# Two transformer blocks on one core: rope, masks and residues move from POOL to DVE, and projections stand ahead of attention

## The chip, the cores and the metric

The kernel runs on one core of a Trainium2 chip. The metric is the time of one execution on the device, in microseconds. Five engines work from queues of their own: PE (TensorE, with PEld for its weight loads), DVE (VectorE), ACT (ScalarE), POOL (GpSimd) and SP (SyncE, which here issues DMAs). An engine takes its instructions in the order of its queue; an instruction that waits holds up all that stand behind it.

## The reference

256 tokens of width 1024 pass through two blocks, all in float32. Block 1 adds a mixer and an MLP:

```python
y_a = sliding_window_sink_attention(q_a, k_a, v_a, attn_sinks) @ w_att_up   # 8 query heads, 2 key heads of 64, window 128
ret = chunkwise_retention(q_r, k_r, v_r)                                    # 4 heads, keys 128, values 256
y_r = (silu(g_r) * head_groupnorm(ret, ret_gn_gain)) @ w_ret_up
merged = sigmoid(gate_a) * y_a + sigmoid(gate_r) * y_r
h = h + merged @ w_out
h = h + square(relu(rmsnorm(h) @ w_ff1)) @ w_ff2
```

Block 2 sees 16 meta tokens ahead of the 256, that is 272 keys:

```python
o_swa = windowed_gqa_sink_attention(qa, ka, va, attn_sink, pos, is_real)    # 16 query heads, 4 key heads of 64
o_diff = differential_attention(qb, kb, vb, lam, lambda_init, gain, is_key) # softmax(q1 k1) - lam softmax(q2 k2), 8 heads
merged = g_swa * (o_swa @ w_branch_swa) + g_diff * (o_diff @ w_branch_diff)
h = h + rms_norm(merged @ w_out, post_mix_gain)
h = h + rms_norm((silu(a) * b) @ w_ffn_out, post_ffn_gain)                  # a, b = u @ w_ffn_in
```

A sink is a logit that takes part in the softmax and has no value. `rope` turns halves of each head by tables of cosines and sines.

## The kernel before

All weights stream as 272 units of 512 KB. `next_unit` and `fetch` load a unit as `raw`, ACT casts it to a rounded part `hi` (L300, two instructions of 128x512) and DVE computes the rest `lo` (L302, two of 128x512); a projection is then 24 matmuls a unit, 8 slices of the depth with `hi` against the rounded activations, `hi` against their rest, and `lo` against the rounded ones (`mm_a`, L456). There are 4 buffers of `raw`, 5 of `hi` and `lo`, and the code takes units one ahead.

`rope_T` (L503 to L513) takes a projection: ACT copies it out, ACT's queue issues DMAs that swap the halves into `sw`, DVE multiplies by the cosines (L509), POOL multiplies `sw` by the sines and adds (L510, L513). `stack_q` (L521 to L524) makes of each query its rounded part (ACT) and its rest (POOL) on two halves of the partitions. `stack_k` (L536 to L539) makes of each key head a tile `ks` with the rounded part on both halves and a tile `kl` with the rest, half by DVE and half by POOL.

`scores` (L546 to L549) gives two matmuls for a score tile `s` and, where there is a mask, one or two more that add a bf16 table through an identity. `sink_softmax` puts the sink into a further column (DVE, L560), takes the row's extreme (L554), the exponential with its sum (ACT, L564), the reciprocal (L566) and the normalised `pn` (DVE, L567). `sink_attention` does this for four heads, transposes them into `pt_ps`, splits that into `pt` (L328 ACT, L329 DVE), multiplies with the values into `o_ps` (L586, which has the single PSUM bank `pv`), and folds that by `ol` and `of` into the output's rounded part and rest.

PSUM has two banks `acc` for projections, two `tp` for transposes, two `s` for scores, one `pv`, and one `x` that joins one of these by phase. A scheduler reorders the instructions as it places them by its own estimates, so the order in the queues is not that of the code. In block 2 the code runs, in this order: values, keys for the window heads, then for each of 4 groups `c` the queries and two `sink_attention`; then for each of 4 pairs `pr` keys, queries, two differential heads and one gate; then, in a phase of its own (`b3`), the first branch product `bs_ps` four times, and four times a gate with the second branch product `bd_ps`. Block 1 runs the retention (four heads: `ra`, `at`, `ro`, `ry`, `yt_ps`), keys and values `kv_ps`, two groups of queries `qa_ps` with two `sink_attention` each, then gates and branch products `au_ps` and `ru_ps`.

## Time and profile before

| | |
|---|---|
| median of 3 runs (lowest, highest) | 917.13 us (916.29, 918.17) |
| the profiled execution | 916.17 us, its span 914.4 us |
| busy: PE, DVE, ACT, POOL | 888.0, 626.2, 516.0, 174.5 us |
| granted clock of TensorE, mean | 0.997 of 2.4 GHz |
| retention and block 1's attention | 33 to 208 us |
| block 2: window attention, differential heads, branch products | 465 to 588, 582 to 657, 612 to 697 us |

PE's matmuls are pipelined: the record of one reaches beyond the start of the next, so a step is read from start to start. A busy share is an average of stages with different limits, so the stages are read one by one.

### The profile page before, as it was taken

What the parts mean: (1) busy time and instruction counts of PE and PEld (TensorE: products, weight loads), DVE (VectorE), ACT (ScalarE), POOL (GpSimd) and SP (SyncE); (2) the same over time, 40 slices, a digit from 0 to 9 for tenths busy, and PEclk for the clock granted to TensorE, in tenths of its full rate; (3) what the DMA queues carried; (4) which work ended last, traced back from release to release, by engine and by line L of the source; (5) the groups of instructions that cost most, each with busy time, mean ns of one, the idle gap of its engine ahead of it and who ended that gap; (6) DMA issues with size and microseconds to landing.
All of it is one profiled execution on the core that took longest, in us unless ns stands there. A gap on an engine that the chain in (4) does not pass through costs nothing. (4 is left out here: it accounts for less than half of the span.)

```text
span 914.4 us, 16482 instructions
## 1 busy us (share of the span) xinstructions
PE 888.0 (97%) x6188; PEld 813.1 (89%) x6188; DVE 626.2 (68%) x1201; ACT 516.0 (56%) x1128; POOL 174.5 (19%) x181
## 2 busy tenths in 40 slices
PE   6999899999999999999989999999999999999997
PEld 4899889998899999987989889899999799999996
DVE  5556889677755555575689999988567675655554
ACT  4544357555655544565657788886455564444442
POOL 3013460101000111101273535451011100000000
PEclk9999999999999999999999999999999999999999
DMA  8675454478565666562664343433457566655551
GB/s 279 237 215 175 147 152 138 125 222 297 166 211 190 195 188 185 186 229 84 204 210 134 110 135 111 136 108 116 139 185 225 213 200 200 190 193 186 185 161 46
DMA packets 48126, 160.18 MB, mean 175 GB/s; under 512 B 6432, under 2 KB 8224, under 8 KB 48048
## 3 DMA queue, kind: packets, MB, share of 16 engines
q1 hardware_dynamic: 43376, 153.95, 53.0%
q10 hardware_dynamic: 4672, 5.20, 2.0%
q8 instruction: 48, 0.79, 0.3%
q14 instruction: 30, 0.25, 0.1%
HBM read 151.83 MB, written 2.10 MB: 168 GB/s over the span
## 5 line engine op out<-in xcount | busy, mean ns | idle before, releaser
L302 DVE TENSOR_TENSOR lo<-raw,hi 128x512 fp32r<-128x512 f32 x536 | 380.3, 751 | 190.8 <-ACT hi L300 187.2
L300 ACT CAST hi<-raw 128x512 fp32r<-128x512 f32 x532 | 301.9, 618 | 239.1 <-issue 81.7
L468 PE MATMUL op<-hi,hid 128*128 128x512 f32 x416 | 130.2, 394 | 0.0
L456 PE MATMUL fi_ps<-xf2t,hi 128*128 128x256 f32 x640 | 113.8, 281 | 0.0
L456 PEld LDWEIGHTS fi_ps<-xf2t,hi 128*128 128x128 f32 x640 | 98.6, 188 | 1.0
L468 PEld LDWEIGHTS op<-hi,hid 128*128 128x128 f32 x416 | 76.3, 188 | 16.1
L456 PE MATMUL fi_ps<-xf2t,lo 128*128 128x256 f32 x320 | 89.7, 280 | 0.0
L468 PE MATMUL op<-lo,hid 128*128 128x512 f32 x208 | 81.7, 394 | 0.0
L456 PE MATMUL f_ps<-xf1t,hi 128*128 128x256 f32 x448 | 80.2, 281 | 0.0
L456 PEld LDWEIGHTS f_ps<-xf1t,hi 128*128 128x128 f32 x448 | 69.5, 188 | 1.3
L456 PE MATMUL f_ps<-xf1t,lo 128*128 128x256 f32 x224 | 62.8, 280 | 0.0
L456 PEld LDWEIGHTS fi_ps<-xf2t,lo 128*128 128x128 f32 x320 | 60.4, 189 | 0.0
L456 PE MATMUL q_ps<-x2t,hi 128*128 128x256 f32 x256 | 50.0, 286 | 0.0
L456 PE MATMUL gate_ps<-x1t,hi 128*128 128x256 f32 x256 | 48.4, 285 | 0.0
L456 PE MATMUL gate_ps<-x2t,hi 128*128 128x256 f32 x256 | 48.4, 284 | 0.0
L468 PEld LDWEIGHTS op<-lo,hid 128*128 128x128 f32 x208 | 39.1, 188 | 8.9
L417 POOL TENSOR_SCALAR e<-ss 128x1 f32<-128x1 f32 (+1 forms) x11 | 4.1, 368 | 221.8 <-ACT py L1030 192.7
L797 POOL TENSOR_TENSOR sq<-relu 128x512 f32<-128x512 f32 x14 | 15.8, 1131 | 150.5 <-ACT relu L794 150.5
L456 PEld LDWEIGHTS f_ps<-xf1t,lo 128*128 128x128 f32 x224 | 42.3, 189 | 0.1
L456 PEld LDWEIGHTS q_ps<-x2t,hi 128*128 128x128 f32 x256 | 40.3, 189 | 0.8 <-issue 0.5
L456 PEld LDWEIGHTS gate_ps<-x2t,hi 128*128 128x128 f32 x256 | 39.8, 188 | 0.6 <-issue 0.5
L456 PEld LDWEIGHTS gate_ps<-x1t,hi 128*128 128x128 f32 x256 | 39.8, 189 | 0.2
(297 smaller groups left out, 2015.6 us busy)
## 6 DMA issues: line engine op xcount, KB each, us to landing
raw<-in_wstream_dram SPq DMA_DIRECT2D x272, 512.0 KB, 3.6
sw<-t ACTq DMA_DIRECT2D x40, 64.0 KB, 3.8
x<-in_x_dram SPq DMA_DIRECT2D x3, 512.0 KB, 6.1
sw<-t ACTq DMA_DIRECT2D x40, 34.0 KB, 2.3
sw<-t ACTq DMA_DIRECT2D x8, 128.0 KB, 3.7
g_pre<-in_gains_dram SPq DMA_DIRECT2D x2, 512.0 KB, 7.1
x<-hf SPq DMA_DIRECT2D x2, 512.0 KB, 2.7
x<-x SPq DMA_DIRECT2D x2, 512.0 KB, 6.2
```

Source lines behind the costliest of these rows:

```text
L300: nc.scalar.copy(hi[:, c:c + PIECE], raw[:, c:c + PIECE])
L302: nc.vector.tensor_sub(lo[:, c:c + PIECE], raw[:, c:c + PIECE], hi[:, c:c + PIECE].bitcast(F32))
L417: nc.gpsimd.tensor_scalar(out=e[:np_], in0=ss[:np_, 0:1], scalar1=1.0 / D, scalar2=EPS, op0=ALU.mult, op1=ALU.add)
L456: nc.tensor.matmul(out, wv[a][:, k, j * P:(j + 1) * P], XT[:, b, k, n0:n1], start=(i == 0), stop=(i == last))
L468: nc.tensor.matmul(out, XT[:, b, k0 + k, t0:t1], wv[a][:, k, c0:c0 + cn], start=(start and i == 0), stop=(stop and i == last))
L797: nc.gpsimd.tensor_tensor(out=q, in0=r, in1=r, op=ALU.mult)
```

## The change

- Masks: the table is now f32 (128x800, 400 KB, loaded ahead of weight unit 4) and holds one row block for each kind of score tile. `scores` has no mask matmuls. One DVE instruction (`tensor_tensor_reduce`) adds the mask to the scores, writes them to `pn` and takes the minimum with the sink as its start; it stands in the order as two rows. The sink's column is a copy on POOL of four columns at a time. The normalisation is on ACT.
- Rope: the multiply by the sines and the add are on DVE. The rests of `stack_q` are on DVE.
- `stack_k`: ACT casts once for a pair of heads into `ku` (one buffer), DVE computes its rest, and four DMAs on POOL's queue (64x544 f32, 139 KB each) copy both into the two stacked tiles. There are 11 such stacks, 10 of them in block 2.
- The copy of half of `o_ps` is two ACT copies of 64x256 in place of one of 64x512.
- Order of the code: the window heads' next queries, and the first pair's keys and queries, are projected ahead of the attention of the present ones; those of pair `pr + 1` after the first differential head of pair `pr`. Each pair now has its first gate, its `bs_ps` and its second gate; that gate is kept in `gd`, in the buffers of `pt`. The phase `b3` is gone, and `bd_ps` stands alone at the end. The units of the weight stream are in the new order.

```diff
-    "b2": dict(vt=4, sw=2, t1=2, t2=2, ks=6, kl=6, qe=2, qo=2, p=6, a=2, at=1, atm=2, y=1, pn=2, pt=2),
-    "b3": dict(gt=4),
+    "b2": dict(sw=2, t1=2, t2=2, ks=8, ku=1, qe=2, qo=2, at=2, atm=2, y=2, pn=3, pt=2),
...
         nc.vector.tensor_mul(t1, raw, C)
-        nc.gpsimd.tensor_tensor(out=sw, in0=sw, in1=S, op=ALU.mult)
+        nc.vector.tensor_mul(sw, sw, S)
...
-        nc.gpsimd.tensor_tensor(out=out, in0=t1, in1=sw, op=ALU.add)
+        nc.vector.tensor_add(out, t1, sw)
...
-        nc.gpsimd.tensor_tensor(out=qe[64:128], in0=qf[0:64], in1=qe[0:64].bitcast(F32), op=ALU.subtract)
+        nc.vector.tensor_sub(qe[64:128], qf[0:64], qe[0:64].bitcast(F32))
...
     def stack_k(self, kf, n):
+        u = self.t([P, 2, n], "ku", F32R)
+        nc.scalar.copy(u[:, 0], kf)
+        nc.vector.tensor_sub(u[:, 1], kf, u[:, 0].bitcast(F32))
         r = []
         for e in range(2):
-            nc.scalar.copy(ks[a], kf[a])
-            nc.scalar.copy(ks[b], kf[a])
-            nc.vector.tensor_sub(kl[a], kf[a], ks[a].bitcast(F32))
-            nc.gpsimd.tensor_tensor(out=kl[b], in0=kf[a], in1=ks[a].bitcast(F32), op=ALU.subtract)
+            ks = self.t([P, 2, n], "ks", F32R)
+            for b in range(2):
+                nc.gpsimd.dma_start(out=ks[64 * b:64 * b + 64].bitcast(F32), in_=u[64 * e:64 * e + 64].bitcast(F32))
...
-        for i, (mi, c0) in enumerate(mask or ()):
-            nc.tensor.matmul(out[:, c0:c0 + P], self.identb, self.masks[:, mi * P:(mi + 1) * P],
-                             start=False, stop=(i == len(mask) - 1))
...
-        nc.vector.tensor_copy(s[:, n:n + 1], nsink)
-        nm = self.row_min(s)
+        nc.vector.tensor_tensor_reduce(out=p[:, :n], in0=s, in1=mask, scale=1.0, scalar=nsink, op0=ALU.add,
+                                       op1=ALU.min, accum_out=nm)
...
-        nc.vector.tensor_scalar(out=out, in0=p[:, :n], scalar1=rc, scalar2=None, op0=ALU.mult)
+        nc.scalar.activation(out=p[:, :n], in_=p[:, :n], func=AF.Copy, scale=rc)
...
         for c in range(4):
-            q = self.stack_q(self.rope_T(self.proj_a(XT, name="q_ps"), 2, NTOK, rope_b, 32, scale=-0.125))
+            if c < 3:
+                nq = queries()
+            else:
+                nk, nq = keys(), queries()
             for qt in range(2):
...
         for pr in range(4):
-            kb = keys()
-            q = self.stack_q(self.rope_T(self.proj_a(XT, name="q_ps"), 2, NTOK, rope_b, 32, scale=-0.125))
+            kb, q = nk, nq
             for m in range(2):
+                self.diff_attention(q, kb[2 * m:2 * m + 2], vb, OD, m, 2 * pr + m)
+                if m == 0 and pr < 3:
+                    nk, nq = keys(), queries()
+            mv = MS[:, 2 * pr:2 * pr + 2, :]
+            self.gate(XT, 16, pr, mv)
+            b = self.proj_a(OS, name="bs_ps")
+            nc.vector.scalar_tensor_tensor(out=mv, in0=mv, scalar=1.0, in1=b, op0=ALU.add, op1=ALU.mult)
+            if pr % 2 == 0:
+                gd.append(self.t([P, 4, NTOK], "gd", tag="pt"))
+            self.gate(XT, 24, pr, gd[-1][:, 2 * (pr % 2):2 * (pr % 2) + 2, :])
```

Three places of the order. First, PE near the end of the window attention. A row is a line of the code, an operation, the tile written and those read (their numbers tell one from another), and a shape. Before, at the products of the last but one group (`o_ps_6124`), with a gate's matmuls between:

```order
L456 MATMUL gate_ps_7414<-x2t_2615,hi166_7217 128x256 x2
L456 MATMUL gate_ps_7414<-x2t_2615,lo166_7218 128x256
L456 MATMUL gate_ps_7414<-x2t_2615,hi167_7415 128x256 x2
L456 MATMUL gate_ps_7414<-x2t_2615,lo167_7416 128x256
L456 MATMUL gate_ps_7414<-x2t_2615,hi167_7415 128x256
L586 MATMUL o_ps_6124<-pt_6150,va_4839 128x512
L582 MATMUL pt_ps_6226<-ident_82,pn_6162 128x128 x4
```

After, at the last but three and the last but two group (`o_ps_5663`, `o_ps_5743`):

```order
L586 MATMUL o_ps_5663<-pt_5689,va_4780 128x512 x2
L582 MATMUL pt_ps_5754<-ident_82,pn_5701 128x128 x4
L582 MATMUL pt_ps_5764<-ident_82,pn_5701 16x128 x4
L547 MATMUL s_6301<-ks_5984,qe_6119 128x272
L548 MATMUL s_6301<-ks_5984,qe_6119 128x272
L957 MATMUL vT_ps_5919<-ident_82,vt_5814 16x128 x2
L957 MATMUL vT_ps_5919<-ident_82,vt_5883 16x128 x2
L547 MATMUL s_6307<-ks_5987,qo_6120 128x272
L548 MATMUL s_6307<-ks_5987,qo_6120 128x272
L586 MATMUL o_ps_5743<-pt_5749,va_4780 128x512 x2
L586 MATMUL o_ps_5743<-pt_5759,va_4780 128x512 x2
L957 MATMUL vT_ps_5925<-ident_82,vt_5814 128x128 x2
```

Where `gate_ps` filled the steps between attention matmuls, scores, transposes of values (`vT_ps`) and products now follow each other.

Second, the first queries of block 2: POOL before, DVE before, then DVE after and POOL after. `t1` and `sw` are the rope's operands, `qe` and `qo` the stacked queries, `kl` and `ku` the rests of keys.

```order
L510 TENSOR_TENSOR sw_5104<-sw_5104,rope_b_4725 128x512
L513 TENSOR_TENSOR t1_5105<-t1_5105,sw_5104 128x512
L510 TENSOR_TENSOR sw_5368<-sw_5368,rope_b_4725 128x512
L513 TENSOR_TENSOR t1_5369<-t1_5369,sw_5368 128x512
L523 TENSOR_TENSOR qe_5115<-t1_5105,qe_5115 64x512
L524 TENSOR_TENSOR qo_5116<-t1_5105,qo_5116 64x512
```

```order
L538 TENSOR_TENSOR kl_5028<-t1_5017,ks_5027 64x272
L538 TENSOR_TENSOR kl_5034<-t1_5017,ks_5033 64x272
L509 TENSOR_TENSOR t1_5369<-t2_5370,rope_b_4725 128x512
L302 TENSOR_TENSOR lo146_5868<-raw146_5869,hi146_5867 128x512 x2
L302 TENSOR_TENSOR lo147_5903<-raw147_5904,hi147_5902 128x512 x2
```

```order
L513 TENSOR_TENSOR sw_4954<-sw_4954,rope_b_4666 128x512
L309 TENSOR_TENSOR lo143_5299<-raw143_5300,hi143_5298 128x512
L516 TENSOR_TENSOR t1_4955<-t1_4955,sw_4954 128x512
L309 TENSOR_TENSOR lo144_5331<-raw144_5332,hi144_5330 128x512 x2
L535 TENSOR_TENSOR ku_4880<-t1_4870,ku_4880 128x272
L526 TENSOR_TENSOR qe_4965<-t1_4955,qe_4965 64x512
L527 TENSOR_TENSOR qo_4966<-t1_4955,qo_4966 64x512
```

```order
L573 COPY pn_5217<-nsink_330 128x4
L573 COPY pn_5379<-nsink_330 128x4
L540 DMA ks_4830<-ku_4827 64x544 x2
L540 DMA ks_4833<-ku_4827 64x544 x2
L540 DMA ks_4883<-ku_4880 64x544 x2
L540 DMA ks_4886<-ku_4880 64x544 x2
```

POOL's rope and rests now stand on DVE among the splits of weights, and POOL has sink copies and the DMAs of keys.

Third, ACT where a gate is evacuated. Before, `ms` from the first gate of block 2; after, `gd` from the second:

```order
L300 CAST hi159_6776<-raw159_6778 128x512 x2
L564 ACTIVATE p_5696,den_5697<-s_5689,mn_5694 128x273
L564 ACTIVATE p_5748,den_5749<-s_5741,mn_5746 128x273
L300 CAST hi160_6808<-raw160_6810 128x512 x2
L602 ACTIVATE ms_4926<-gate_ps_6596,hb_330 128x256 x2
L589 COPY ol_5469<-o_ps_5438 64x512
```

```order
L606 ACTIVATE p_6815,den0_6813<-s_6816,mn_6819 128x272
L335 CAST os_t_4781<-of_6198 128x2x128
L628 COPY at_6326<-at_ps_6321 128x512
L606 ACTIVATE p_6815,den1_6814<-s_6822,mn_6825 128x272
L335 CAST pt_6273<-pt_ps_6268 16x512
L663 ACTIVATE gd_6745<-gate_ps_6746,hb_326 128x256 x2
L633 COPY atm_6331<-atm_ps_6328 16x256
L606 ACTIVATE p_6815,den0_6813<-s_6828,mn_6831 128x272
L606 ACTIVATE p_6815,den1_6814<-s_6834,mn_6837 128x272
```

The gate's two instructions now stand behind the last small cast into `pt`.

## Rows read from the trace of the kernel before

**Rows 1.** The page's first part: the busy time of each engine, its share of the span of 914.4 us, and its instructions.

```profile
PE 888.0 (97%) x6188; PEld 813.1 (89%) x6188; DVE 626.2 (68%) x1201; ACT 516.0 (56%) x1128; POOL 174.5 (19%) x181
```

**Rows 2.** Busy time in stretches, from:to in us; the columns are length, then busy us (and instructions) of PE, PEld, DVE, ACT and POOL, the granted clock of TensorE as a share of 2.4 GHz, the DMA share and GB/s. The stretches are the retention with the first queries, the first part of the window attention, and a stretch of branch products with no attention in it.

```profile
85.00:113.00 28.00, 24.62 (x180) 23.61 (x179) 19.67 (x39) 10.87 (x21) 12.95 (x14) 0.94 0.51 163
465.00:490.00 25.00, 22.59 (x175) 21.03 (x174) 22.82 (x51) 16.51 (x41) 16.33 (x11) 1.00 0.55 166
660.00:697.00 37.00, 37.00 (x317) 37.00 (x316) 23.70 (x32) 18.62 (x35) 4.80 (x3) 1.00 0.61 185
```

**Rows 3.** PE's timeline inside the window attention; the columns are start (us), length (us; of a matmul its modelled end, so the step is from one start to the next), engine, line, operation, tiles, shape and count.

```profile
504.15 0.29 PE L547 MATMUL s<-kl,qo 128*128 128x272 f32 x1
504.28 0.23 PE L549 MATMUL s<-masksb,identb 128*128 128x128 bf16 x1
504.32 0.37 PE L546 MATMUL s<-ks,qe 128*128 128x272 f32 x1
504.53 0.29 PE L547 MATMUL s<-kl,qe 128*128 128x272 f32 x1
...
506.58 0.50 PE L586 MATMUL o_ps<-pt,va 16*128 16x512 f32 x1
507.01 0.65 PE L582 MATMUL pt_ps<-ident,pn 128*128 128x128 f32 x4
507.42 0.36 PE L456 MATMUL q_ps<-x2t,hi 128*128 128x256 f32 x1
```

**Rows 4.** PE's waits from 438 to 660 us, all of them: who waited for whom, us in total, times, the longest.

```profile
PE o_ps L586 <- DVE of L592: 1.6, 2, 1.4
PE s L546 <- ACT p L564: 1.5, 2, 0.8
PE k_ps L456 <- ACT ms L602: 1.2, 1, 1.2
PE vb_ps L456 <- ACT vt L890: 0.5, 1, 0.5
PE s L546 <- POOL qo L524: 0.4, 1, 0.4
```

**Rows 5.** PE's waits from 85 to 210 us, all of them, in the same columns.

```profile
PE ro L691 <- DVE at L687: 2.4, 1, 2.4
PE yt_ps L706 <- DVE ry L701: 1.9, 2, 1.1
PE va_ps L724 <- DVE va L329: 0.8, 1, 0.8
```

**Rows 6.** DVE's instructions from 438 to 660 us by line and shape; count, then busy us and mean ns of one, then idle time before them and its releasers.

```profile
L302 DVE TENSOR_TENSOR lo<-raw,hi 128x512 fp32r<-128x512 f32 x99 | 83.2, 872 | 10.0 <-ACT hi L300 9.9
...
L554 DVE TENSOR_REDUCE mn<-s 128x1 f32<-128x273 f32 x32 | 13.1, 428 | 0.1
L538 DVE TENSOR_TENSOR kl<-t,ks 64x272 fp32r<-64x272 f32 x20 | 12.5, 625 | 4.2 <-ACT ks L536 3.9
L567 DVE TENSOR_SCALAR pn<-p,rc 128x272 f32<-128x272 f32 x32 | 12.2, 410 | 0.2
L329 DVE TENSOR_TENSOR pt<-pt_ps,pt 128x512 fp32r<-128x512 f32 x16 | 10.8, 678 | 0.1
...
L592 DVE TENSOR_TENSOR of<-o_ps,ol 64x256 f32<-64x256 f32 x16 | 6.6, 411 | 0.2
L509 DVE TENSOR_TENSOR t<-t,rope_b 128x512 f32<-128x512 f32 x8 | 6.1, 757 | 1.3 <-POOL qo L524 1.2
...
L509 DVE TENSOR_TENSOR t<-t,rope_b 128x272 f32<-128x272 f32 x10 | 5.0, 505 | 1.7 <-ACT t L503 1.7
...
L560 DVE COPY s<-nsink 128x1 f32<-128x1 f32 x32 | 4.2, 147 | 0.1
```

**Rows 7.** The same view of 720 to 900 us, where POOL has 4 instructions.

```profile
L302 DVE TENSOR_TENSOR lo<-raw,hi 128x512 fp32r<-128x512 f32 x124 | 80.0, 688 | 62.7 <-ACT hi L300 62.7
```

**Rows 8.** The timeline of 469 to 476 us, POOL and DVE.

```profile
472.93 1.80 POOL L510 TENSOR_TENSOR sw<-sw,rope_b 128x512 f32<-128x512 f32 x1
...
473.50 3.48 DVE L302 TENSOR_TENSOR lo<-raw,hi 128x512 fp32r<-128x512 f32 x2
```

**Rows 9.** POOL's costliest rope instruction from 438 to 660 us.

```profile
L510 POOL TENSOR_TENSOR sw<-sw,rope_b 128x512 f32<-128x512 f32 x8 | 13.1, 1634 | 30.0 <-DMA sw<-t 19.8 <-DVE pt L329 5.6 <-DVE of L592 4.0
```

**Rows 10.** ACT's instructions from 438 to 660 us.

```profile
L300 ACT CAST hi<-raw 128x512 fp32r<-128x512 f32 x98 | 55.7, 618 | 8.9 <-PE bs_ps L456 2.9 <-PE gate_ps L456 2.1 <-DMA raw<-in_wstream_dram 1.4
L941 ACT ACTIVATE p<-s,mn 128x272 f32<-128x272 f32 x32 | 15.6, 488 | 9.0 <-DVE mn L554 8.8
...
L328 ACT CAST pt<-pt_ps 128x512 fp32r<-128x512 f32 x16 | 9.2, 588 | 2.4 <-issue 1.3 <-PE k_ps L456 0.7
...
L589 ACT COPY ol<-o_ps 64x512 f32<-64x512 f32 x8 | 4.7, 583 | 1.1 <-ACT t L503 0.6 <-PE o_ps L586 0.3
...
L328 ACT CAST pt<-pt_ps 16x512 fp32r<-16x512 f32 x8 | 4.5, 566 | 1.2 <-PE pt_ps L582 0.8 <-issue 0.4
```

**Rows 11.** DVE's timeline in the retention; in brackets the idle time before, and what ended it.

```profile
91.57 0.54 DVE L701 TENSOR_SCALAR ry<-ro,mv,rq 128x256 f32<-128x256 f32 x1 [4.06 <-POOL rq L400]
...
103.39 0.42 DVE L509 TENSOR_TENSOR t<-t,rope_a 128x256 f32<-128x256 f32 x1 [2.56 <-DMA rope_a<-in_consts_dram]
```

**Rows 12.** The page's DMA issues: tile, queue, count, KB each, median us to landing.

```profile
sw<-t ACTq DMA_DIRECT2D x8, 128.0 KB, 3.7
```

More of the change, by code (lines that the diff above doesn't have):

```diff
@@ L126, in pack_weights @@
     for p in range(4):
-        in_a(w_in2, o_kb + 256 * p)
-        in_a(w_in2, o_qb + 256 * p)
+        if p < 3:
+            kq(p + 1)
         in_a(w_in2, o_g + 256 * p)
+        in_a(w_bs, 256 * p)
+        in_a(w_in2, o_g + 1024 + 256 * p)
     for g in range(4):
-        in_a(w_bs, 256 * g)
-    for g in range(4):
-        in_a(w_in2, o_g + 1024 + 256 * g)
         in_a(w_bd, 256 * g)
@@ L184, in make_consts @@
     j = np.arange(P)[None, :]
-    add("masks", np.concatenate([np.where(j <= i, 0.0, MASKED), np.where(j >= i, 0.0, MASKED),
-                                 np.where(j > i, 0.0, MASKED)], axis=1))
+    le, ge, gt = (np.where(c, 0.0, MASKED) for c in (j <= i, j >= i, j > i))
+    z = np.zeros((P, P))
+    add("masks", np.concatenate([gt, le, z, le, z[:, :NMETA], ge, z, z[:, :NMETA]], axis=1))
     f = _freqs(500000.0, 16)
@@ L364, in consts2 @@
         cc = _CC
-        mk = self.wp.tile([P, UP], F32, tag="raw", bufs=4, name="mk")[:, 0:3 * P]
-        a, n = cc["masks"]
-        nc.sync.dma_start(out=mk, in_=io["consts"][:, a:a + n])
-        self.identb = cp.tile([P, P], BF16, name="identb")
-        self.masks = cp.tile([P, 3 * P], BF16, name="masksb")
-        nc.gpsimd.tensor_copy(self.identb, self.ident)
-        nc.gpsimd.tensor_copy(self.masks, mk)
+        mk = self.load("masks", [P, 2 * P + 2 * NKEY])
+        self.mask1 = [mk[:, P:2 * P], mk[:, 0:2 * P]]
+        self.mask2 = [mk[:, 2 * P:2 * P + NKEY], mk[:, 2 * P + NKEY:]]
         self.vec = cp.tile([P, 48], F32, name="vec")
@@ L885, in v_T @@
             vt = []
-            for _ in range(m):
+            for j in range(m):
                 b = self.acc([P, NKEY], name)
                 self.mm_a(b, self.next_unit(), XT, 0, NKEY)
-                f = self.t([P, NKEY], "vt")
-                nc.scalar.copy(f, b)
-                vt.append(f)
+                if j % 2 == 0:
+                    f = self.t([P, 2, NKEY], "vt", tag="ks")
+                nc.scalar.copy(f[:, j % 2], b)
+                vt.append(f[:, j % 2])
             for i, (a, z) in enumerate(toks):
@@ L916, in block2, with queries @@
         self.banks("WINDOW")
+        def queries():
+            return self.stack_q(self.rope_T(self.proj_a(XT, name="q_ps"), 2, NTOK, rope_b, 32, scale=-0.125))
         ka = keys()
+        q = queries()
+        for i, b in v_T(2, "va_ps"):
+            v = vat[:b.shape[0], i]
+            self.split(v[:, :, 0:64], v[:, :, 64:128], b.rearrange("p m (h d) -> p (m h) d", h=2))
+            va[i] = v
+        va = [va[1], va[2], va[0]]
         for c in range(4):
-            q = self.stack_q(self.rope_T(self.proj_a(XT, name="q_ps"), 2, NTOK, rope_b, 32, scale=-0.125))
+            if c < 3:
+                nq = queries()
+            else:
+                nk, nq = keys(), queries()
             for qt in range(2):
-                self.sink_attention(q, ka[c], va, self.nsink[:, 8:24], kts, [(0, P)] if qt == 0 else [(1, 0)],
-                                    OS, c, qt)
+                self.sink_attention(q, ka[c], va, self.nsink[:, 8:24], kts, self.mask2[qt], OS, c, qt)
+            q = nq
             if c == VB1:
@@ L998, in block2 @@
+            nc.vector.scalar_tensor_tensor(out=mv, in0=mv, scalar=1.0, in1=b, op0=ALU.add, op1=ALU.mult)
+            if pr % 2 == 0:
+                gd.append(self.t([P, 4, NTOK], "gd", tag="pt"))
+            self.gate(XT, 24, pr, gd[-1][:, 2 * (pr % 2):2 * (pr % 2) + 2, :])
         self.banks("BRANCH")
-        for gq in range(4):
-            b = self.proj_a(OS, name="bs_ps")
-            mv = MS[:, 2 * gq:2 * gq + 2, :]
-            nc.vector.scalar_tensor_tensor(out=mv, in0=mv, scalar=1.0, in1=b, op0=ALU.add, op1=ALU.mult)
@@ L1003, in block2 @@
         MT = self.big("C", 8, "m2t")
         for gq in range(4):
-            tg = self.t([P, 2, 2, NTOK], "gt")
-            self.gate(XT, 24, gq, tg[:, 0])
+            g = gd[gq // 2][:, 2 * (gq % 2):2 * (gq % 2) + 2, :]
             b = self.proj_a(OD, name="bd_ps")
-            nc.vector.scalar_tensor_tensor(out=tg[:, 1], in0=tg[:, 0], scalar=1.0, in1=b, op0=ALU.add, op1=ALU.mult)
-            nc.gpsimd.tensor_tensor(out=tg[:, 0], in0=tg[:, 1], in1=MS[:, 2 * gq:2 * gq + 2, :], op=ALU.add)
@@ L1010, in block2 @@
[L1010 removed]
+            nc.vector.scalar_tensor_tensor(out=g, in0=g, scalar=1.0, in1=b, op0=ALU.add, op1=ALU.mult)
+            nc.vector.tensor_add(g, g, MS[:, 2 * gq:2 * gq + 2, :])
+            self.split(MT[:, 0, 2 * gq:2 * gq + 2, 0:NTOK], MT[:, 1, 2 * gq:2 * gq + 2, 0:NTOK], g, 0.5)
         es.close()
```

181 lines of the change are left out of this document (85 added, 96 removed).

## The prediction

> **What bounds the kernel now.** I first read the busy line, then the busy time by stretch, then the waits of PE. PE is busy for 888 of 914.4 us [rows 1], and a stretch with nothing but branch products shows its pace: 317 matmuls in 37.00 us, 0.117 us each [rows 2]. So the kernel is bound by PE nearly everywhere, and a change can only gain in three ways: matmuls that go, waits of PE that go, and waits that it does not put in their place. The reader should see how little there is. All waits of PE from 438 to 660 us add to 5.2 us in 8 waits [rows 4], and those from 85 to 210 us to 5.1 us in 4 [rows 5]. Each is counted from the modelled end of the matmul before it, 0.28 us long, while the next one can start 0.12 us after its start [rows 2, 3], so each is short by some 0.16 us: 6.5 and 5.7 us.
>
> What stands behind the waits in the window attention is DVE. It is busy for 22.82 of 25 us from 465 to 490 us [rows 2], and part of that is no work: its split of a weight piece takes 872 ns there and 688 ns where POOL is idle [rows 6, 7]. The timeline shows the pair: two such splits take 3.48 us while POOL multiplies and subtracts from SBUF [rows 8], against 1.38 us for two at the later mean.
>
> **The change, part by part.** *Masks off PE.* 56 mask matmuls go. In the timeline the step onto the matmul behind a mask is 0.04 us, but the step after that is 0.21 us where the same matmul without a mask ahead takes 0.13 us [rows 3]. One mask so costs 0.04 + 0.08 = 0.125 us, and 56 of them 7.0 us, 24 in block 1 (3.0) and 32 in block 2 (4.0). They are on PE's own queue, so this is the surest term: **-7.0**. The mask and the sink now come in one DVE instruction with the minimum, plus a short one that writes it. No row shows it. It replaces the minimum (428 ns) and the sink's copy (147 ns) [rows 6]; I take 428 ns for it and nothing for the short one, and keep double as the other end, 32 x 0.43 = 13.7 us more of DVE.
>
> *POOL's work to DVE.* From 438 to 660 us DVE loses 99 x (872 - 688) ns = 18.2 us of blocked splits, 12.5 us of key residues, 12.2 us of normalisation (now on ACT) and 4.2 us of sink copies [rows 6, 7]: 47 us. It gains 16 rope instructions of 128x512 at 757 ns, 20 of 128x272 at 505 ns, 16 query residues at no more than 757 ns and 10 key residues at 505 ns: 12.1 + 10.1 + 12.1 + 5.1 = 39 us, prices of an engine that POOL still disturbed [rows 6]; in the ratio 688 to 872 they would be 31. So DVE is relieved by only 8 to 16 us of 222, and stays some 85% busy. I therefore let half of the 6.5 us of waits go: **-3.2**, with 0 and -6.5 as ends. The rope chain itself gets shorter, since the 1.63 us multiply on POOL [rows 9] becomes one of at most 0.76 us.
>
> *Block 1.* The waits for `ry` and `va` are POOL's doing: DVE sat 4.06 us until POOL had raised a variance to a power, behind rope work on its queue [rows 11]. POOL now has that queue nearly to itself, so 1.9 + 0.8 us in 3 waits [rows 5] go, with 3 x 0.16 us: **-3.2**. The largest wait, 2.4 us for `at`, stays: `at` is queued on DVE behind the rope product that waits 2.56 us for the load of `rope_a` [rows 11], and the order after has the same product ahead of the same `at`; the load's buffer still comes free only with the last add of the rope before. Its row also shows a granted clock of 0.94 in 85 to 113 us [rows 2], so after that wait some matmuls ran at the lower level of 1.2 GHz; that stays too. The mask table is now 400 KB ahead of weight unit 4 and no longer 192 KB behind unit 8; 208 KB at the 163 GB/s of a quiet stretch [rows 2] are 1.3 us, perhaps hidden by the start's other loads: **+0.7**.
>
> *The new order.* Here the profile of before cannot show the gain as such, but the order shows a cost. Before, the last window groups and the first differential scores stand among keys, queries and gates. After, keys and queries of pairs 0 and 1 and two gates have been used up before them, and one stretch follows, from the transposes of `pn_5621` to `k_ps_6882`, with hardly any projection. Both `acc` banks are held: `bs_ps` needs all window heads, and `gate_ps_6746` cannot be evacuated, since its `gd` tile takes a `pt` buffer that frees after the last window group. On PE it holds 13 score pairs (26 x 0.125), 62 transposes (0.41 us for four [rows 3]), 16 `o_ps` matmuls with 128 partitions (twice a 256-column one, 0.23) and 7 with 16 (0.43 [rows 3]), and 12 of `bs_ps`: 3.3 + 6.4 + 3.7 + 3.0 + 1.4 = 17.8 us. On ACT it holds 14 exponentials (488 ns), 4 normalisations (0.41, their price on DVE), 10 copies of 128x512 and one `at` (588), 4 of 16x512 (566), 8 half copies of `o_ps` (half of 583), 4 casts of 128x256 (0.41) and a key, a query and a gate part (1.5 us together) [rows 6, 10]: 6.8 + 1.6 + 6.5 + 2.3 + 2.3 + 1.6 + 1.5 = 22.6 us, some 7% less when they follow each other, since a busy time overlaps the next: 21. ACT is later by 3.3 us at least. At most the four `o_ps` groups run as a chain through the single `pv` bank: cast 0.59, residue 0.68, four products 0.92, small cast and residue 1.25, two products 0.86, two copies and adds 1.4, 5.7 us each, with the 6.8 us of exponentials between them: 29.6 - 17.8 = 11.8 us. The chain and the sum share the same ACT, so I take the middle, **+7**, and keep 3 and 12. Behind it, two further products of keys among waiting scores: 0 to 2, **+1**. From there on gates, `bs` and later projections stand among the differential heads, as many matmuls as before, and the waits of before name none of the differential heads' products [rows 4]: 0. POOL's 40 copies of keys in block 2 must land before scores; keys are projected a pair ahead, which hides them (rival below).
>
> The sum: -7.0 - 3.2 - 3.2 + 0.7 + 7 + 1 = -4.7 us on the profiled execution. That took 916.17 us (1.8 us outside the span), 0.96 below the median of 917.13, so the forecast is 916.2 - 4.7 + 1.0 = **912.5 us**.
>
> **Rivals.** *The order costs nothing much.* DVE without POOL runs so much ahead that all 6.5 us of waits go and the dense stretch costs its floor: -7.0 - 6.5 - 3.2 + 0.7 + 3.3 = -12.7, 904.4 us. For it: DVE idles 10 us for ACT even now [rows 6], so it is a matter of queue order as much as of load.
>
> *The dense stretch decides (slower).* Place: between the last window groups and `k_ps_6882`; price: the chain of 12 us, 2 behind it, and no wait won before, since DVE's load is hardly lower: -7.0 - 3.2 + 0.7 + 12 + 2 = +4.5, 921.6 us. It turns the sign once the stretch costs over 11.7 us with half the old waits gone, or 8.4 with none. For it: DVE still 85% busy, two weight banks both held. Against: ACT has only 21 us to do there.
>
> *The fused minimum takes two passes.* Then DVE has 13.7 us more, which eats the relief; DVE sets block 2's pace, and the 4.0 us of masks there are hidden: -3.0 - 3.2 + 0.7 + 7 = +1.5, 918.6 us, no change that can be told.
>
> *The copies of keys land late.* The row of 128 KB on ACT's queue lands in 3.7 us [rows 12]; a copy here is 139 KB and four of them follow on POOL's queue. In pairs, 7.4 us. `ku` has one buffer, and ACT's next cast into it waits for all four, with weight casts and exponentials behind it. Between two such casts ACT has as little as two exponentials, six weight casts and some small ones, about 5 us: 2.4 us of ACT's wait for each of five second stacks, 12 us, of which a third falls into ACT's idle third (16.51 of 25 us busy [rows 2]): +8, 920.5 us. The Trainium skill, "SBUF — State Buffer", section "SBUF: two separate sides", speaks for this rival: a DMA issued by GpSimd cannot get its descriptors written while DVE runs an operation that takes the shared port pair. No row of before has such a DMA. "DMA: Bandwidth & Descriptors", section "Anatomy of one DMA — SWDGE (gpsimd) path", fits 2.0 us plus bytes over 436e3 per us; by it a copy is an estimated 2.3 us and this rival would cost nothing.
>
> **How the numbers follow.** Forecast 0.42 (its own range 908 to 917), order free 0.22, dense stretch 0.16, two passes 0.10, late keys 0.10. About 0.2% (1.8 us: 915.3 to 919.0) is what a measurement of this kernel can tell from no change. Faster: 0.30 of the forecast's chance, the second case, 0.01 of the last: 0.53. Same: 0.12 of the forecast's, 0.08 of two passes, 0.02 of the last: 0.22. Slower: the rest, 0.25. The range from 901 to 924 reaches below the second case and above the third.
>
> **What the profile after would show.** Masks: no bf16 matmul, and the step after a score pair at 0.12 to 0.13 us. POOL: weight splits near 690 ns in the window attention; if they stay at 870, something else holds DVE. Block 1: no wait for `ry`, and the wait for `at` still there. Dense stretch: PE waiting for ACT and DVE in many short steps for 3 to 12 us in one place of some 25 us, after a wait-free start of block 2; if PE is over 95% busy there, the second case holds. Two passes: a masked minimum near 860 ns. Late keys: ACT idle before `ku` with a POOL DMA as releaser. The forecast is wrong if the dense stretch does not show, or if waits appear that the order does not name.

## The result, and the profile of the changed kernel

The changed kernel takes 925.42 us (median of 6 runs, 922.41 to 927.16) against 918.36 us (6 runs, 916.29 to 920.10): ratio 1.0068, 95% interval 1.0049 to 1.0087. It is slower by 0.7%, just above the range of the prediction, which ended at 924. Its profiled execution, at 925.45 us, is a typical one with a span of 923.4 us; the profiled one of the kernel before took 916.17, 2.2 below its median, so the spans differ by 9.0 us and the medians by 7.1. The page's busy line:

```profile
PE 888.9 (96%) x6132; PEld 813.5 (88%) x6132; DVE 608.5 (66%) x1216; ACT 523.3 (57%) x1155; POOL 82.8 (9%) x139
```

The edits did what they say: 56 matmuls are gone (the masks came to DVE from PE, not from POOL as in the title), and POOL has half its work [rows 1]. Yet PE's busy time did not fall: part of it now runs at a lower granted clock, 0.986 over the span, where the kernel before has 0.997.

Busy time in stretches, with the columns of [rows 2]: the retention, the start of block 2, and the end of the window attention.

```profile
85.00:113.00 28.00, 28.00 (x233) 27.74 (x232) 20.86 (x44) 11.68 (x22) 6.00 (x10) 1.00 0.65 201
440.00:449.00 9.00, 0.67 (x6) 0.45 (x4) 4.64 (x9) 4.12 (x9) 0.00 (x0) 0.74 0.71 203
449.00:470.00 21.00, 20.85 (x156) 20.79 (x157) 13.11 (x38) 12.88 (x36) 2.04 (x4) 0.87 0.40 123
541.00:573.00 32.00, 26.83 (x129) 19.26 (x127) 23.73 (x62) 24.17 (x65) 3.42 (x7) 0.79 0.22 64
```

Block 1 got what was forecast and more: PE is busy for all of 85 to 113 us, at full clock. Block 2 has two holes. The longest of PE's waits from 400 to 700 us, as in [rows 4]:

```profile
PE vT_ps L957 <- ACT vt L952: 8.5, 1, 8.5
PE s L547 <- DVE mn L560: 2.1, 4, 0.9
PE o_ps L586 <- DVE of L592: 2.0, 2, 1.3
PE s L547 <- ACT p L606: 1.3, 2, 0.8
PE pt_ps L582 <- DVE pt L336: 1.1, 2, 0.6
```

The first is a single wait of 8.5 us, at 440 us. It is followed back in two timelines of the changed kernel, DVE's and then ACT's (in brackets the idle time before, and what ended it; ACTq are the DMAs that ACT issues):

```profile
445.50 0.69 DVE L513 TENSOR_TENSOR sw<-sw,rope_b 128x512 f32<-128x512 f32 x1 [3.67 <-DMA sw<-t]
446.11 0.68 DVE L309 TENSOR_TENSOR lo<-raw,hi 128x512 fp32r<-128x512 f32 x1
446.71 0.68 DVE L516 TENSOR_TENSOR t<-t,sw 128x512 f32<-128x512 f32 x1
```

```profile
436.00 0.59 ACT L508 ACTIVATE t<-q_ps 128x512 f32<-128x512 f32 x1
...
437.81 1.81 ACTq L510 DMA_DIRECT2D sw<-t  x1
...
439.66 0.79 ACTq L511 DMA_DIRECT2D sw<-t  x1
...
442.94 0.42 ACT L534 CAST ku<-t 128x272 fp32r<-128x272 f32 x1 [0.27 <-DMA ks<-ku]
447.43 0.62 ACT L524 CAST qe<-t 64x512 fp32r<-64x512 f32 x1 [4.07 <-DVE t L516]
448.07 0.62 ACT L525 CAST qo<-t 64x512 fp32r<-64x512 f32 x1
448.71 0.67 ACT L952 COPY vt<-va_ps 128x272 f32<-128x272 f32 x2
```

PE's transposes need the values' copies `vt`. These stand on ACT behind the queries' casts, which wait for DVE's last rotary add, which waits for the swap's DMA. From the copy of the queries (436.0 us) to DVE's multiply (445.5) the swap takes 9.5 us; the issue of its four DMAs on ACT's queue alone lasts from 436.6 to 440.5. The new order puts the first keys and queries ahead of the values (the section on the change does not list this), so the first queries' whole rotary chain lies on PE's path, and for 21 us behind it the granted clock is 0.87.

DVE by line from 440 to 700 us, as in [rows 6] (the last line is the second, short part of the fused instruction), and after it DVE's longest sort of wait from 400 to 700 us:

```profile
L309 DVE TENSOR_TENSOR lo<-raw,hi 128x512 fp32r<-128x512 f32 x117 | 76.1, 683 | 10.0 <-ACT hi L307 9.0 <-DMA raw<-in_wstream_dram 0.5
L560 DVE CUSTOM_DVE_ANT_0 pn<-s,masks,nsink 128x272 f32<-128x272 f32 x32 | 15.0, 489 | 0.6 <-PE s L548 0.6
...
L513 DVE TENSOR_TENSOR sw<-sw,rope_b 128x512 f32<-128x512 f32 x8 | 5.5, 689 | 12.1 <-DMA sw<-t 12.1
...
L560 DVE DVE_READ_ACCUMULATOR2_ANT mn<- 128x1 f32 x32 | 2.5, 79 | 0.0
```

```profile
DVE sw L513 <- DMA sw<-t: 19.0, 11, 3.7
```

The splits run at 683 ns, as forecast. But DVE now waits for the swaps: 12.1 us ahead of the eight multiplies of queries, where POOL had 19.8 [rows 9], and 19.0 us in 11 waits ahead of all 18, with minima and splits queued behind them. In the same window the kernel before had more of this wait, but on POOL:

```profile
POOL sw L510 <- DMA sw<-t: 60.5, 9, 28.5
```

### The profile page after: what moved, and what is told of

The parts are those of the page before. It is cut to its first block, busy times and chain, and to the rows that moved or that the text cites. A ratio compares the mean times of both kernels' runs of the same rounds, so it can differ in the third digit from the quotient of the medians.

```text
span 923.4 us, 16358 instructions
## 1 busy us (share of the span) xinstructions
PE 888.9 (96%) x6132; PEld 813.5 (88%) x6132; DVE 608.5 (66%) x1216; ACT 523.3 (57%) x1155; POOL 82.8 (9%) x139
## 5 line engine op out<-in xcount | busy, mean ns | idle before, releaser
L309 DVE TENSOR_TENSOR lo<-raw,hi 128x512 fp32r<-128x512 f32 x536 | 351.2, 695 | 180.0 <-ACT hi L307 176.5
L459 PEld LDWEIGHTS fi_ps<-xf2t,lo 128*128 128x128 f32 x320 | 60.5, 189 | 0.0
L459 PE MATMUL q_ps<-x2t,lo 128*128 128x256 f32 x128 | 37.3, 291 | 0.0
L459 PE MATMUL gate_ps<-x1t,lo 128*128 128x256 f32 x128 | 36.1, 282 | 0.0
```

What stands on the lines that cost most here:

```text
L309: nc.vector.tensor_sub(lo[:, c:c + PIECE], raw[:, c:c + PIECE], hi[:, c:c + PIECE].bitcast(F32))
L459: nc.tensor.matmul(out, wv[a][:, k, j * P:(j + 1) * P], XT[:, b, k, n0:n1], start=(i == 0), stop=(i == last))
```

## The experiments

The table has, for each kernel, the start of `vb_ps` (end of block 1), the time from there to the start of the first `fi_ps` (block 2), and this time in three parts, from windows of 5 us: *idle* (length less PE's busy time), *clock* (busy time multiplied by one less the granted clock) and *rest*, PE's work at full clock. The stages are those of one profiled execution, which lies up to 2.5 us from its kernel's median; the changed kernel, e1, e2 and e3, with the same code in block 1, end it at 403.2 to 405.6. So a difference of some 2 us between two stages says little. The last two columns are of all runs.

| kernel | end of block 1 | block 2 | idle | clock | rest | median | ratio, 95% |
|---|---|---|---|---|---|---|---|
| before | 413.4 | 307.3 | 5.8 | 0.0 | 301.5 | 918.4 | 1 |
| after | 404.2 | 323.8 | 16.6 | 8.5 | 298.7 | 925.4 | 1.0049–1.0087 |
| e1 values first | 405.6 | 320.0 | 11.5 | 10.1 | 298.4 | 922.2 | 1.0023–1.0057 |
| e2 and own gate slot | 403.2 | 315.2 | 10.5 | 4.3 | 300.5 | 917.3 | 0.9966–0.9988 |
| e3 old order, new operations | 404.4 | 327.6 | 17.0 | 11.7 | 298.9 | 929.6 | 1.0086–1.0127 |
| e4 before + masks | 410.9 | 315.5 | 12.8 | 2.9 | 299.8 | 924.6 | 1.0040–1.0092 |
| f1 after, rotary on POOL | 408.9 | 320.7 | 17.5 | 4.8 | 298.3 | 926.8 | 1.0070–1.0102 |
| f2 after, no swaps | 402.6 | 307.9 | 6.8 | 3.2 | 297.8 | 908.2 | 0.9864–0.9896 |
| f3 before + rotary on DVE | 406.6 | 309.5 | 4.6 | 4.7 | 300.2 | 911.7 | 0.9903–0.9949 |
| f4 = e3, rotary on POOL | 410.2 | 317.6 | 12.4 | 6.3 | 298.9 | 922.6 | 1.0029–1.0058 |
| g1 = f3 + masks in block 1 | 404.9 | 310.3 | 4.8 | 4.6 | 300.9 | 911.4 | 0.9898–0.9951 |
| g2 = g1, no masks in block 2 | 404.5 | 311.9 | 10.7 | 1.7 | 299.4 | 912.5 | 0.9913–0.9959 |
| g3 = g1 + fused in block 2 | 403.7 | 315.7 | 8.0 | 5.8 | 301.9 | 916.3 | 0.9962–0.9991 |
| g4 after, block 2's masks on PE | 402.0 | 321.7 | 16.2 | 2.1 | 303.4 | 923.0 | 1.0027–1.0106 |
| h1 = e2 + g4 | 405.6 | 311.3 | 9.0 | 0.0 | 302.3 | 916.0 | 0.9952–0.9995 |
| h2 after, keys by copies | 402.8 | 316.3 | 11.9 | 4.5 | 299.9 | 916.0 | 0.9958–0.9988 |
| h3 = h1 + h2 | 404.2 | 324.0 | 14.2 | 7.1 | 302.6 | 922.8 | 1.0033–1.0058 |

The theory was that block 2 loses by waits which the new order and the moved rotary work put on PE's path; the first rival was the dense stretch of the new order alone.

**e1**, the values ahead of keys and queries (and their weight units likewise):

```diff
-        ka = keys()
-        q = queries()
         for i, b in v_T(2, "va_ps"):
...
         va = [va[1], va[2], va[0]]
+        ka = keys()
+        q = queries()
```

> The changed kernel with one thing moved: in block 2 the window heads' values are projected ahead of the first keys and queries, as before the change. Theory (the order of the code lost the time in two places): the 8.6 us wait of the values' transposes for ACT goes, and with it the low granted clock behind it (0.87 over 21 us, 2.7 us): 925.4 - 11.3, about 914 us; the stretch without projections further on stays. Rival (the copies of keys on POOL's queue crowd the DMA engines, so that the swaps land late wherever the values stand): the wait only moves to the first scores, 921 us or more.

The wait for `vt` is gone, and the start is at full clock, but the time is 922.2 us and not the theory's 914, and block 2 gains only 3.8 us: idle falls by 5.1, and the dense stretch now loses more to the clock. Windows of e1:

```profile
449.00:470.00 21.00, 20.85 (x168) 20.26 (x167) 16.93 (x34) 14.89 (x32) 2.05 (x4) 1.00 0.81 238
541.00:573.00 32.00, 28.72 (x132) 21.18 (x133) 23.13 (x64) 23.38 (x66) 3.16 (x7) 0.73 0.12 27
```

**e2**, e1 and a slot of its own for the first gate's result, so that the gate's bank can be emptied while the window heads still hold the `pt` slots:

```diff
-                gd.append(self.t([P, 4, NTOK], "gd", tag="pt"))
+                gd.append(self.t([P, 4, NTOK], "gd", tag="gd" if pr == 0 else "pt"))
```

(`at` and `y` of block 2 go from two buffers to one, for space.)

> As e1_values_first, and the first pair of kept gates has a buffer of its own in place of one of pt (at and y have one buffer each to make room), so that the second gate need not wait for the last window group. Theory (the stretch without projections is long because that gate holds a bank of PSUM): the stretch gets shorter, the granted clock stays at 1 there, some 7 us less than e1_values_first: about 907 us. Rival (the stretch is set by the chain of four window groups through one bank): the same time as e1_values_first within 2 us.

Another 4.8 us of block 2: the clock's part falls from 10.1 to 4.3, while PE's work reads 2.1 more. The same window in e2 is nearly filled, and most of its clock is back:

```profile
541.00:573.00 32.00, 30.96 (x211) 27.26 (x212) 26.43 (x59) 23.93 (x62) 5.11 (x10) 0.95 0.53 159
```

So the held gate bank was part of the dense stretch's cost, as the prediction had read from the order. The two steps of e2 take the changed kernel from 925.4 to 917.3 us, just below the kernel before: they undo the loss.

**e3**, all new operations in the code order of before (the values come first in it too):

```diff
-            if c < 3:
-                nq = queries()
-            else:
-                nk, nq = keys(), queries()
+            q = queries()
...
+            kb, q = keys(), queries()
```

> The changed kernel's instructions with the old order of the code in block 2: values, keys, then queries just ahead of their attention; one gate per pair; the first branch products and second gates at the end. Theory (the moves of work from POOL to DVE and of the masks are a gain, the order is the loss): block 1 keeps its 9 us, block 2 gains masks (4.0) and half of its waits (3): 918.4 - 16, about 902 us. Rival (DVE or the copies of keys are the loss): 918 us or more, with waits for DVE or for the copies in the window attention.

It is slower than the changed kernel, where the theory had 902 us. So the new order is not the loss as such: with these operations it is the better of the two.

**e4**, the kernel before with the masks' edit alone:

```diff
-        nm = self.row_min(s)
+        nc.vector.tensor_tensor_reduce(out=p[:, :n], in0=s, in1=mask, scale=1.0, scalar=nsink, op0=ALU.add,
+                                       op1=ALU.min, accum_out=nm)
```

(no mask matmuls; block 1's `qe` goes from three buffers to two)

> The kernel before with only the masks changed: no mask matmuls, mask and minimum in one DVE instruction, the sink's column copied into the exponential's tile by DVE as before (the queries' first tile has 2 buffers in block 1 in place of 3, to make room). Theory (a mask matmul costs PE 0.125 us, 56 of them 7.0 us): 911 to 913 us, a little less gain than 7.0 where DVE sets the pace. Rival (DVE sets the pace in the window attention and the fused instruction takes two passes): 917 us or more.

Block 1 gains 2.5 us, block 2 loses 8.2. The two longest of PE's waits from 400 to 700 us:

```profile
PE s L544 <- DVE mn L558: 5.5, 3, 2.5
PE o_ps L583 <- DVE of L589: 2.2, 2, 1.8
```

PE's work shrinks by 1.7, but idle grows by 7.0: DVE, busy for 113.1 of the 115 us from 465 to 580 us, now holds the score banks.

**f1**, **f3** and **f4** move only the rotary multiply and add, in the changed kernel and e3 back to POOL, in the kernel before to DVE (f3's edit shown):

```diff
-        nc.gpsimd.tensor_tensor(out=sw, in0=sw, in1=S, op=ALU.mult)
+        nc.vector.tensor_mul(sw, sw, S)
...
-        nc.gpsimd.tensor_tensor(out=out, in0=t1, in1=sw, op=ALU.add)
+        nc.vector.tensor_add(out, t1, sw)
```

> The changed kernel with the rope's multiply by the sines and its add back on POOL. The first experiments sank the theory of the order alone: with the old order the changed instructions are slower still. New theory: on DVE the multiply waits for the swap's transfer with all of DVE's queue behind it (19.0 us in 11 waits from 410 to 700 us in the changed kernel; before, POOL waited there, 60 us, and nobody behind it): those waits go and 6 to 9 us with them, 916 to 919 us, though POOL's rope slows DVE's splits again. Rival (POOL in DVE's way costs more than the waits): 925 us or more, splits above 800 ns.

> The kernel before with only the rope's multiply by the sines and its add moved from POOL to DVE. Theory (the moved wait is the loss): DVE shows waits for the swap's transfers in block 2 of 15 us or more, and the time is 923 to 929 us, although the splits get faster. Rival (POOL off the shared memory is worth more): 915 us or less.

> The changed instructions in the old order of block 2, with the rope back on POOL. Theory (moved waits): 929.6 - 12, about 917 us, below e3_old_order by more than f1 is below the changed kernel, since in the old order the queries are projected just ahead of their attention. Rival (the old order is slow with the changed instructions for another reason, such as the masked minimum on DVE or the copies of keys): 925 us or more.

f1 missed its theory of 916 to 919 us: with the multiply back on POOL the changed kernel takes 926.8. PE's long wait at the start of block 2 is still there, now for the stacked query `qe`:

```profile
PE s L547 <- DVE qe L526: 8.4, 1, 8.4
```

So the swap's delay lies on PE's path in this order, whichever engine multiplies. f3 missed its theory of 923 to 929 us by more. It is faster than both kernels, 0.9926, and DVE waits little for the swaps from 400 to 700 us, where POOL had 60.5:

```profile
DVE sw L510 <- DMA sw<-t: 5.8, 6, 1.8
```

A wait does not simply move along with its instruction. It fits that DVE is fuller in f3 (111.3 of 115 us from 465 to 580 us, against 92.9 in e3, which waits 22.4 us for swaps) and so comes to the multiply later; that was not tested apart.

f3 takes block 1 from 413.4 to 406.6 us, and its window shows why: the wait for `at` and the lower clock of [rows 2] are gone.

```profile
85.00:113.00 28.00, 28.00 (x227) 27.58 (x226) 24.23 (x50) 12.86 (x26) 6.70 (x10) 1.00 0.56 163
```

In block 2 the same edit costs 2.2 us alone, 3.1 in the changed kernel (f1 to after) and 10.0 among the new operations in the old order (f4 to e3). Only the last is well clear of the spread, and there the medians agree: 922.6 to 929.6 us, although block 1 gains.

**f2**, the changed kernel without the swaps' DMAs: the rotary's second term is made from the unswapped copy, so the rotation is left out.

```diff
-            nc.scalar.dma_start(out=sw[p:p + half], in_=raw[p + half:p + 2 * half])
-            nc.scalar.dma_start(out=sw[p + half:p + 2 * half], in_=raw[p:p + half])
...
-        nc.vector.tensor_mul(sw, sw, S)
+        nc.vector.tensor_mul(sw, raw, S)
```

> The changed kernel without the swap's transfers: the multiply by the sines reads the unswapped copy, so rope is not computed; every instruction of DVE stays. Theory (the waits for the swaps, not DVE's added work, are the loss): the wait of the values' transposes (8.6 us) and most of the 19 us of DVE's waits go, the dense stretch stays: 925.4 - 12, about 913 us. Rival (DVE's added work, 31 to 39 us in block 2, is the loss): 921 us or more.

Block 2 falls by 15.9 us to 307.9, as long as before: without the swaps nearly all that it lost is back. This takes away the chain of the first queries, DVE's waits, and the DMAs' issue on ACT (32 + 40 of them), so it bounds the swaps' price in this order, not that of DVE's waits alone. The kernel before was not run without its swaps.

**g1 to g3** start from f3. g1 fuses the masks in block 1 alone; g2 leaves out block 2's masks altogether; g3 puts the fused instruction, with a table of zeros, in the place of block 2's reduction and keeps the matmuls.

```diff
-                self.sink_attention(q, ka[c], va, self.nsink[:, 8:24], kts, self.mask2[qt],
-                                    OS, c, qt)
+                self.sink_attention(q, ka[c], va, self.nsink[:, 8:24], kts, None,
+                                    OS, c, qt, [(0, P)] if qt == 0 else [(1, 0)])
```

(g1 against e4 with f3's edit; with `None` the reduction is used. g2 has `None` for the list of matmuls too; g3 has a table in the place of the first `None`.)

> The kernel before with the rotary multiply and add on DVE and the fused mask and minimum in block 1 alone; the 32 window attentions of block 2 keep their mask matmuls and the plain reduction (queries' even buffers of block 1 go from 3 to 2, as in the run with masks alone). Theory (the mask edit pays in block 1 and costs in block 2): block 1 keeps both gains (end of block 1 at about 404.2, before 413.4), block 2 takes what it took with the rotary work alone on DVE (about 309.5), the whole about 909 us, 9 below the kernel before. Rival (what the mask edit costs does not depend on the block, and the 8.2 us of block 2 in the run with masks alone were its queries' two buffers, or the table): the whole at 915 or more.

> As the run with masks fused in block 1 and rotary work on DVE, but block 2's window attention has no mask at all (left out: the 32 mask matmuls, and nothing in their place; the plain reduction stays). It prices the matmuls alone. Prediction's term: 32 at about 125 ns, 4.0 us less than that run, so about 905. Theory (DVE sets the pace of the window attention, the matmuls stand beside its work): at most 1.5 us less, so 907.5 to 910.

> As the run with masks fused in block 1 and rotary work on DVE, but block 2's window attention has the fused instruction (with a table of zeros) in the place of the reduction, and keeps the 32 mask matmuls; so the fused instruction alone is added. Theory (the fused instruction paces the scores, since it keeps the score bank until DVE has read it, and costs more DVE time than the reduction and the copy of the sink): 6 to 10 us more than that run, so 915 to 919. Prediction's own reckoning (0.57 us fused against 0.58 for reduction and copy): within 1 us of it, about 909.

g1: block 1 ends 1.7 us sooner than in f3, but the medians, 911.4 and 911.7, can't be told apart, so the theory's 909 was missed; the rival's 915 too. g2 answers the prediction's surest term: without the 32 matmuls PE has 1.5 us less work, 5.9 us more idle time and 2.9 less of clock, and the kernel is not faster (912.5). That DVE's queue makes this idle time fits its load, 112.2 of 115 us from 465 to 580 us; PE's own waits name POOL's `qe`, DVE's `y` and ACT's `p`, so it is argued and not shown. g3: the fused instruction alone costs 4.9 us, a little under the theory's 6. By DVE's lines in g3 it is no slower than what it replaces:

```profile
L575 DVE CUSTOM_DVE_ANT_0 p<-s,masks,nsink 128x272 f32<-128x272 f32 x32 | 15.4, 488 | 0.0
...
L572 DVE COPY p<-nsink 128x1 f32<-128x1 f32 x26 | 3.5, 142 | 0.0
L575 DVE DVE_READ_ACCUMULATOR2_ANT mn<- 128x1 f32 x32 | 2.6, 81 | 0.0
```

It is 0.57 us with its short second part, against 428 + 147 ns [rows 6]; but in this form the sink's copy stays on DVE, so DVE has 21.5 us of this work (26 of the 32 copies are in the row) where g1's reductions and copies take 13.5 + 4.6 = 18.1. How the rest of the 4.9 us comes about is not settled.

**g4**, the changed kernel with block 2's masks back on PE (the same edit in `after`).

> The changed kernel with the masks of block 2's window attention put back on PE (mask matmuls, sink's copy into the score bank, plain reduction); block 1 and all else as changed. Theory (the mask edit costs about 8 us in block 2 in any order of the work): block 2 takes about 316 us, the whole about 917. Rival (the mask edit cost only beside normalisation on DVE and POOL's rotary work, which the changed kernel does not have there): within 2 us of the changed kernel, 923 to 927; by the prediction's term even 4 us more, 929.

Block 2 takes 321.7, not the 316 of the theory: in the changed kernel the masks cost 2.1 us there. The intervals of g4 and the changed kernel overlap. It fits that what the fused instruction costs depends on what else DVE has: most in e4, where normalisation is on DVE and POOL disturbs it.

**h1** takes e2 and g4 together. **h2** is the changed kernel with the keys' halves made by engines, not by POOL's DMAs (`a` is the half of the partitions on which a key head already lies, `b` the other); **h3** is both.

```diff
-            for b in range(2):
-                nc.gpsimd.dma_start(out=ks[64 * b:64 * b + 64].bitcast(F32), in_=u[64 * e:64 * e + 64].bitcast(F32))
+            nc.scalar.copy(ks[a, 0], kf[a])
+            nc.scalar.copy(ks[b, 0], kf[a])
+            nc.vector.tensor_sub(ks[a, 1], kf[a], ks[a, 0].bitcast(F32))
+            nc.gpsimd.tensor_tensor(out=ks[b, 1], in0=kf[a], in1=ks[a, 0].bitcast(F32), op=ALU.subtract)
```

> The changed kernel with the values ahead of keys and queries, the branch gate's own slot for the first pair, and the masks of block 2's window attention back on PE. If these costs are separate (3.8 + 4.8 + 2.1 us of block 2 by their own runs): block 2 takes 323.8 - 10.7 = 313.1 us, the whole about 915. Rival (one wait that each of them exposes in turn): no better than the run with values and gate alone, 917.3 or more.

> The changed kernel with the keys' stacked halves made as before, by two ACT copies and a subtraction each on DVE and POOL, in the place of the 40 DMAs from POOL's queue; all else as changed. Theory (the DMAs are hidden, 4.0 us from issue to landing a pair or more ahead of use; the copies add about 20 operations of 0.3 to 0.5 us to ACT and 10 to 20 to DVE and POOL): 925 to 931. Rival (late keys, which the prediction priced at some 8 us): 918 to 922.

> The edits of the two runs above together: what then stays of the change is block 1's mask edit, the rotary work on DVE, the normalisation on ACT, and the new order. If the costs add up: the first of the two runs plus the difference that the second makes to the changed kernel, so 915 to 920 by the theory that the keys' DMAs are hidden, 908 to 912 by the rival.

h1's block 2 came out near the sum of its parts, 311.3 (expected 313.1), with no clock loss left. Its median, 916.0 us, lies between the theory's 915 and the rival's 917.3, and its interval overlaps that of e2: that the masks give anything beyond e2 is not shown. h2 missed the theory by 9 us and fell below the rival's 918. Its ACT timeline says why:

```profile
441.36 0.37 ACT L953 COPY vt<-va_ps 128x272 f32<-128x272 f32 x1
...
443.84 0.37 ACT L953 COPY vt<-va_ps 128x272 f32<-128x272 f32 x1
...
446.89 0.62 ACT L524 CAST qe<-t 64x512 fp32r<-64x512 f32 x1 [0.83 <-DVE t L516]
```

With the keys made by copies, ACT's queue has the values' copies ahead of the queries' casts, and the wait of 8.5 us is 0.8 us. In h3, where the values are first anyway, the same copies cost 6.8 us against h1. So the keys' DMAs are not what the change loses by; h2 removed the same wait as e1, through the order on ACT's queue. That they crowd the swaps is not seen either: a swap of 64 KB lands in 4.4 us in the changed kernel, and without the keys' DMAs in 3.6 (h2) and 4.3 (h3), all medians, and DVE still waits 15.1 and 16.8 us for swaps there. Why its dense stretch also keeps more of the clock than e1's is open.

## Why the prediction was wrong

**Where it stands.** Block 1 was forecast at -5.5 us (-3.0 masks, -3.2 waits, +0.7 table) and came out at -9.2; block 2 at +0.8 (-4.0 - 3.2 + 7 + 1) and came out at +16.5: PE's work -2.8, idle +10.8, clock +8.5. Signs within block 1 were right; block 2 turned the result. Behind it, to the end of the span, come another +1.7 us, for which the sum had no term; their cause is open.

In block 2 the two holes hold 22.2 of the 25.1 us of idle time and clock: the start, 440 to 470 us, 11.4, where the sum had nothing, and the dense stretch 10.8, where it had 7. The rest has 2.9 us, where all of block 2 before had 5.8. So by the changed kernel's own account PE's work (-2.8 for the masks' -4.0) and the waits elsewhere (-2.9 for -3.2) came near the forecast, and the step that failed by most is the start of block 2. The experiments add that the masks' term was not a gain that could be counted on.

**Masks, -7.0, "the surest term".** Block 1's 3.0 is confirmed in kind (-2.5 in e4, -1.7 from f3 to g1). Block 2's 4.0 is a step that failed too. The matmuls are on PE's queue, but DVE is nearly full there [rows 2], and in the kernel with the old order PE's time comes back as idle time (g2), while the fused instruction adds 4.9 us (g3) or, with all of e4, 8.2. In the changed kernel, too, the matmuls put back cost nothing that can be told (g4). The price of the instruction was too low: 428 ns and nothing for its second part, where it takes 489 + 79 ns, which is 4.5 us more of DVE in 32. That its place in a full queue decides was not costed. The rival of two passes had it right that block 2's masks bring nothing, for a reason that did not occur, and its 918.6 us is 7 us too low.

**Relief of DVE, -3.2.** The working compared busy times: splits at 688 ns (683 measured), 39 us in, 47 out. The relief came, and was larger than forecast: from 438 to 660 us DVE is busy for 190.1 us before and for 164.7 after. (The 85% of the working is the share before; 8 to 16 us less would have left 78 to 82%. And [rows 4] hold 7 waits, not 8, which makes 6.3 us of 6.5.) The two windows, before and after:

```profile
438.00:660.00 222.00, 216.56 (x1657) 199.86 (x1656) 190.11 (x424) 161.24 (x417) 90.71 (x80) 1.00 0.45 137
438.00:660.00 222.00, 206.06 (x1508) 189.12 (x1507) 164.70 (x399) 154.38 (x397) 26.50 (x49) 0.95 0.51 152
```

Away from the two holes the waits fell about as forecast (above). What failed is the step from load alone to waits: the working left out that the instruction moved from POOL is one that *waits*, and in the new order DVE stands for 19.0 us ahead of minima and splits. All that the swaps cost in block 2 is bounded by f2, 15.9 us. Their move to DVE costs 3.1 of it by f1, within the spread; 10.0 in the old order with the new operations (e3), and 2.2 with the old ones (f3).

**"A wait-free start of block 2".** Wrong, and the largest single step: a wait of 8.5 us, with the clock behind it 11.4 us, where the sum had nothing. The order shows `vt` behind `qe` and `qo` on ACT; the prediction followed PE's order into the dense stretch and not ACT's at the place where keys and queries were moved ahead of the values.

**Dense stretch, +7 (3 to 12).** Place and kind were right: 541 to 573 us. Full-clock work there is 26.83 x 0.79 = 21.2 of 32 us, so it costs 10.8: 5.2 of idle time, within what was sized, and 5.6 of clock, which was not in the sum. Moving the first gate off the shared slot (e2) gave 4.8 back, nearly all clock. The rival in which this stretch decides (921.6 us) came nearest, in part by luck: it had the place and the sign, but 12 us for the stretch and 2 behind it, and nothing for the start of block 2.

**Block 1's waits, -3.2.** `va` is gone, as forecast, and `ry` went from 1.9 to 0.8 us, where the forecast had none. PE's waits from 85 to 210 us, all of them:

```profile
PE yt_ps L767 <- DVE ry L762: 0.8, 1, 0.8
```

The wait for `at` "stays" was wrong: it went, and the clock of 0.94 with it. So 3.7 us of block 1's gain were not foreseen. f3 shows that the rotary work on DVE alone does this (-6.8 us), e4 without it keeps both (2.2 us for `at`, clock 0.94). It fits that the add of the rope before, which frees the table's buffer [rows 11], is off POOL's queue; that was not tested apart.

**Late keys.** ACT waited 0.27 us for the keys' DMAs where shown above and nowhere else in block 2, POOL's 44 issues took 0.52 us in the median and 0.79 at most, and h3 speaks against the rival. The time of a transfer was longer than by the page cited: "DMA: Bandwidth & Descriptors" of the Trainium skill, section "Anatomy of one DMA — SWDGE (gpsimd) path", gives an estimated 2.3 us, and the profile of the changed kernel has a median of 4.0 us. The measurement decides.

```profile
ks<-ku POOLq DMA_DIRECT2D x40, 136.0 KB, 4.0
```

**The sum again**, from one-part runs: block 1 -9.2. Block 2 gives back 3.8 (values first), 4.8 (gate slot) and, in h1's one profiled execution, 3.9 with the masks on PE: 12.5 of 16.5. The rest, 4.0, belongs to what h1 keeps (the new order, the keys' DMAs, the rotary work and rests on DVE, the normalisation on ACT) and was not split further. The version to keep is f3 or g1, 911.4 to 911.7 us: rotary work on DVE, and the old order with block 2's masks on PE.

## What to carry to other kernels

Before moving an instruction to another engine, look at what it waits for, and at when the new queue will come to it: 60.5 us of waits on POOL became 5.8 on DVE in f3, where the move was a gain, and 22.4 in e3, where it was a loss. On an in-order queue such a wait stops all that is behind. Matmuls taken off PE are worth their time only where PE sets the pace; where its partner is full, they can come back as idle time. When work is projected ahead, follow each engine's queue at the new place, ACT's above all, for a short copy that now stands behind a long chain.
